# First two weights in quarters on the ScalarE queue, last output product on VectorE, two W_out pieces noted later

## The chip, the cores and the metric

One NeuronCore of a Trainium2 chip runs the whole program; the other cores are not used. The metric is the device time of one execution in microseconds (us). A profiled execution gives the trace that the tables below come from. TensorE is called PE here, its weight loads PEld, VectorE DVE, ScalarE ACT, GpSimd POOL and SyncE SP. A name with a q behind it (SPq, ACTq) is the queue side of that engine: instructions that issue a DMA. Line numbers L... are those of the kernel before.

## The reference, cut to what matters

Two transformer blocks run one after the other on x of 512 tokens by 1024 channels, fp32. Sizes of the gated feed-forward are 1024 to 2816 and back, those of the squared-ReLU one 1024 to 4096 and back.

```
def swiglu_ffn(x, w_gate, w_up, w_down):
    return (jax.nn.silu(x @ w_gate) * (x @ w_up)) @ w_down

def first_block(x, ...):
    x = x + 0.5 * swiglu_ffn(rmsnorm(x, ffn1_norm), ffn1_w_gate, ffn1_w_up, ffn1_w_down)
    x = x + hybrid_mixer(rmsnorm(x, mix_norm), ...)
    x = x + 0.5 * swiglu_ffn(rmsnorm(x, ffn2_norm), ...)
    return rmsnorm(x, final_norm)

def second_block(x, ...):
    h = rmsnorm_2(x, norm_mix_pre)
    ...
    mixed = jnp.concatenate([o_diff, o_mlstm], axis=-1) @ w_out
    x = x + rmsnorm_2(mixed, norm_mix_post)
    h = rmsnorm_2(x, norm_mlp_pre)
    u = jnp.square(jax.nn.relu(h @ w_up))
    return x + rmsnorm_2(u @ w_down, norm_mlp_post)
```

The change touches three places: the very first products (x @ ffn1_w_gate and x @ ffn1_w_up of the first block), the sum with w_out of the second block, and the last lines, rmsnorm_2(u @ w_down, norm_mlp_post) and the final sum.

## The kernel before

**Products.** Every fp32 product of two matrices is made of three products of the rounded type fp32r: high part by high part, low by high, high by low. So every operand is split in two. For a weight, ACT copies the raw tile `wraw` into `whi` and DVE subtracts to get `wlo` (`split`); for an activation ACT makes `xh` and DVE `xl`. One weight tile is 128 partitions by 1024 numbers (512 KB). There are 3 raw buffers (`R_BUFS`) and 4 split ones (`W_BUFS`); the list `L` (`plan`) holds all weight tiles in the order in which they are used, `w_load` issues their loads on SP's queue and `w_pump` (L448) notes the splits of tile i and the load of tile i + 3. The first two tiles, i = 0 (gate) and i = 1 (up), are split in two halves each (`step = m // 2 if i < 2`).

**Order of work.** The program is not issued as it is written. Every operation is noted (`Program.note`), and `issue` then plans: a list scheduler with estimated costs runs 60 sweeps forwards and backwards with some noise, keeps the best plan, and sends the operations to the engines sorted by planned start. Each engine then runs its own list strictly in order, and waits only where an operation's inputs are not ready or its buffer is still in use. A DMA is such an operation too, in the list of the engine on whose queue it is issued. All noted operations have the line of one helper, L232, in the profile, so they are told apart by their tiles here. DMA completions are counted in 8 semaphores (DMAHW0 to DMAHW7 below) that SP's and ACT's DMAs take by turns in issue order; a DMA that takes one again first waits until the former DMA of that semaphore has landed.

**The head** (L580 to 590 and `first_norm`). x comes in 8 pieces m of 128 channels (256 KB each, `XT<-x`); the gain of the first norm comes as `rows1` on ACT's queue. POOL builds the identity; PE makes 8 transposes of it and one of rows1. For every x piece, PE makes 4 transposes into a bank, ACT makes xh, DVE xl, and ACT or DVE copies the piece to X. The products of the first feed-forward need xh, xl of a piece and whi, wlo of the weight. The norm's scale is put in later, so the products need not wait for it.

```
for half in range(2):
    for m in range(4 * half, 4 * half + 4):
        load_x(m)
        if m == 4 * half:
            for i in range(2):
                k = slice(m, m + 4)
                self.sp.dma_start(self.w_view(self.raw[i], i)[:, k, :], self.L[i][1][:, k, :])
```

**The mLSTM heads** (L1231 to 1235). `scores(h)` and `value(h)` make head h; `o2a(j)` is the share of the diff-attention heads in the j-th pieces of the sum with w_out. These pieces are filler for PE between the heads.

**The tail** (`mlp_phase`, L1338 on). The last half of the output is made for one block of 128 tokens after the other, t = 0 to 3; the last block is cut into two pieces of 256 columns (p1, p2). `post` adds a piece to y (DVE), squares and sums it (ACT) and multiplies it by the gain (POOL). Then a short chain of 128x1 operations makes the norm's factor (cv on DVE, Ln and Exp on ACT, ct, ct, a2f on DVE), and DVE makes the last sum, `XT<-X,a2f,XT`, which SP stores.

Of the kernel before, what the change touches and what calls it, by code (L numbers as in the profile page):

```python
# [13 lines left out]
ALU = mybir.AluOpType  # L14
# [5 lines left out]
NT = 4  # L20
KD = 8
# [293 lines left out]
class Kern:  # L315
# [132 lines left out]
    def w_pump(self, upto):  # L448
        while self.w_split < min(upto + 1, len(self.L)):
            i = self.w_split  # L450
            self.w_load(i + R_BUFS)
            m = self.L[i][2] * self.L[i][3]
            step = m // 2 if i < 2 else m
            for c in range(0, m, step):
                c = slice(c, c + step)
                self.split(self.wh[i % W_BUFS][:, c], self.wl[i % W_BUFS][:, c], self.raw[i % R_BUFS][:, c])
            self.w_split += 1
            self.w_load(self.w_split + R_BUFS)
# [91 lines left out]
    def setup(self):  # L550
        tc, I, ctx = self.tc, self.I, self.ctx
        cp = ctx.enter_context(tc.tile_pool(name="cp", bufs=1))
        pp = ctx.enter_context(tc.tile_pool(name="pp", bufs=1, space=bass.MemoryType.PSUM))
        self.B = [pp.tile([P, 512], F32, name=f"bank{i}") for i in range(8)]
        self.mmb = Rot(self.B)
        dp = ctx.enter_context(tc.tile_pool(name="dp", bufs=1, space=bass.MemoryType.DRAM))
        self.tape = dp.tile([8, 16, 384], F32, name="tape")

        T = lambda name, shape, dt=F32: cp.tile(shape, dt, name=name)
        self.w_init(cp)  # L560
        self.X, self.XT = T("X", [P, KD, S]), T("XT", [P, NT, D])
        self.xh, self.xl = T("xh", [P, KD, S], F32R), T("xl", [P, KD, S], F32R)
        self.xs = [(self.xh[:, m, :], self.xl[:, m, :]) for m in range(KD)]
        self.ident, self.onesr = T("ident", [P, P]), T("onesr", [P, P], F32R)
        self.hm2 = T("hm2", [P, 2])
        self.rows1, self.rows, self.cols = T("rows1", [8, P]), T("rows", [NROW, P]), T("cols", [P, 8 + NROW])
        self.rcol = T("rcol", [P, NT])
        self.cv, self.ct, self.cr = (T(n, [P, 16]) for n in ("cv", "ct", "cr"))
        self.gfp = T("gfp", [P, KD])
        self.rsb, self.acc = T("rsb", [P, S]), T("acc", [P, S])  # L570
        self.sqh, self.sql = T("sqh", [P, S], F32R), T("sql", [P, S], F32R)
        self.sq = Rot([T(f"sq{i}", [P, S]) for i in range(2)])

        def load_x(m):
            self.sp.dma_start(self.XT[:, :, m * P:(m + 1) * P],
                              I["x"][0][:, m * P:(m + 1) * P].rearrange("(t p) c -> p t c", p=P))
        self.ac.dma_start(self.rows1, I["ffn1_norm"][0].rearrange("(r c) -> r c", c=P))
        self.po.memset(self.ident, 1.0)
        for s in (1, -1):
            self.po.affine_select(out=self.ident, in_=self.ident, pattern=[[s, P]], base=0, channel_multiplier=-s,  # L580
                                  compare_op=ALU.is_ge, fill=0.0)
        for half in range(2):
            for m in range(4 * half, 4 * half + 4):
                load_x(m)
                if m == 4 * half:
                    for i in range(2):
                        k = slice(m, m + 4)
                        self.sp.dma_start(self.w_view(self.raw[i], i)[:, k, :], self.L[i][1][:, k, :])
        self.w_dma = 2
        self.w_load(R_BUFS)  # L590
        self.prog.table(LN_EXP)
        self.act(self.onesr, self.ident, AF.Copy, scale=0.0, bias=1.0)
        self.ci = {"g1": 0}
        r = 0
        for name, src, n in [
            ("gm", I["mix_norm"][0], 8), ("g2", I["ffn2_norm"][0], 8),
            ("gf", I["final_norm"][0], 8), ("gp", I["norm_mix_pre_2"][0], 8), ("gu", I["norm_mlp_pre_2"][0], 8),
            ("psc", I["pool_scale"][0], 4), ("cb", I["conv_b_2"][0], 4), ("dn", I["diff_norm_2"][0], 1),
        ]:
            self.po.dma_start(self.rows[r:r + n, :], src.rearrange("(r c) -> r c", c=P))  # L600
            self.ci[name] = 8 + r
            r += n
        self.po.dma_start(self.rows[r:r + 16, :], I["conv_w_2"][0].rearrange("j (r c) -> (j r) c", c=P))
        self.ci["cw"] = 8 + r
        r += 16
        self.po.dma_start(self.rows[r:r + 4, :], I["mlstm_norm_2"][0])
        self.ci["ln"] = 8 + r
        r += 4
        for nm, key in (("qn", "q_norm"), ("kn", "k_norm")):
            for d in range(2):  # L610
                self.po.dma_start(self.rows[r:r + 1, d * 64:(d + 1) * 64], I[key])
            self.ci[nm] = 8 + r
            r += 1
        assert r == NROW
        self.po.dma_start(self.hm2, I["k_hm2"])
# [514 lines left out]
    def mlstm_phase(self):  # L1130
        I = self.I
        with self.mem.scope() as T:
# [22 lines left out]
            for t in range(NT):  # L1155
                b = self.bank()
# [15 lines left out]
            def o2a(i):  # L1172
                w = self.W(("o2A", i))
                for hf in range(2):
                    b = self.bank()
                    self.fgroup(b, w, o_x, hf * P)
                    self.act(y[:, 2 * i + hf, :], b, AF.Copy)
# [53 lines left out]
                self.split(*hls[i][1], self.mk[:, i, :])  # L1231
            scores(0), mo(0), mo(1), mo(2), mo(3), value(0)
            scores(1), o2a(0), o2a(1), value(1)
            scores(2), o2a(2), o2a(3), value(2)
            scores(3), value(3)
            self.y = y

    def mlp_phase(self):
        I = self.I
        X, y = self.X, self.y  # L1240
        with self.mem.scope() as T:
            uh, ul = T([P, 8, S], F32R), T([P, 8, S], F32R)
            rr = Rot([T([P, S]) for _ in range(2)])
            gp = T([P, D])
# [12 lines left out]
            b = self.bank()  # L1257
# [5 lines left out]
            for a in range(2):  # L1263
                cols = slice(a * H2, (a + 1) * H2)
                acc = self.acc[:, cols]
                for m in range(KD):
                    b = self.bank()
# [3 lines left out]
                b = self.bank()  # L1271
# [3 lines left out]
                for m in range(KD):  # L1275
                    t, xm = tmp.next(), X[:, m, cols]
# [21 lines left out]

            y = X[:].rearrange("p m s -> p (m s)").rearrange("p (t d) -> p t d", t=NT)

            def post(t, cs_, b, part):

                yt = y[:, t, cs_]
                self.tt(yt, b, yt, ALU.add)
                self.act(junk[:, cs_], yt, AF.Square, accum_out=ss[:, part, t:t + 1])
                self.tt(yt, yt, gp[:, cs_], ALU.mult, self.po)

            us = [(uh[:, m, :], ul[:, m, :]) for m in range(8)]
            for c in range(4):
# [9 lines left out]
                for m in range(lead, 8):  # L1319
                    b = self.bank()  # L1320
# [17 lines left out]
            for t in range(NT):  # L1338
                cuts = [(S, S)] if t < NT - 1 else [(S, H2), (S + H2, H2)]
                for i, (c0, n) in enumerate(cuts):  # L1340
                    b = self.bank()[:, :n]
                    self.tgroup(b, ww, us, t, slice(c0 - S, c0 - S + n))
                    post(t, slice(c0, c0 + n), b, 1 + i)
                    if len(cuts) > 1 and i == 0:
                        self.tt(s01[:, t:t + 1], ss[:, 0, t:t + 1], ss[:, 1, t:t + 1], ALU.add)
                cc = slice(t, t + 1)
                v, r, w = self.cv[:, cc], self.cr[:, cc], self.ct[:, cc]

                if len(cuts) > 1:
                    self.stt(v, ss[:, 2, cc], s01[:, cc], f5[:, cc], ALU.add, ALU.mult)  # L1350
                else:
                    self.stt(v, ss[:, 0, cc], ss[:, 1, cc], f5[:, cc], ALU.add, ALU.mult)
                self.act(tl[:, cc], v, AF.Ln, bias=eps)
                self.act(r, tl[:, cc], AF.Exp, scale=-0.5)
                self.act(yv[:, cc], r, AF.Copy, scale=v3[:, cc])
                self.stt(w, v, EPS, r, ALU.add, ALU.mult)
                self.stt(w, w, -0.5, r, ALU.mult, ALU.mult)
                self.stt(f4[:, cc], w, 1.5, yv[:, cc], ALU.add, ALU.mult)
                step = S if t < NT - 1 else H2
                for c0 in range(0, D, step):  # L1360
                    xt = self.XT[:, t, c0:c0 + step]
                    self.stt(xt, y[:, t, c0:c0 + step], f4[:, cc], xt, ALU.mult, ALU.add)
                    self.sp.dma_start(self.out[0][t * P:(t + 1) * P, c0:c0 + step], xt)
# [66 lines left out]
```

## Time and profile before

| | |
|---|---|
| median of 3 runs | 1520.19 us (1520.16 to 1520.71) |
| profiled execution, its own time | 1518.48 us |
| span of the profiled execution | 1516.8 us |
| PE busy | 1496.4 us, 99% of the span |
| DVE busy | 797.4 us, 53% |
| ACT busy | 629.5 us, 42% |
| POOL busy | 256.6 us, 17% |
| DMA | 156.10 MB, 103 GB/s on average |

The span goes from the first to the last instruction; the rest of the execution's time lies around it. Matmuls are pipelined: the duration of one record is longer than the distance to the next one, and a stretch of dense records counts as busy throughout. Idle time of an engine that nobody waits for costs nothing.

### The profile page before, as it was taken

To read this page: it belongs to the slowest core of one execution; us is meant where nothing else is said; L and a number is where in the kernel's file an instruction comes from. 1 tells how busy PE (TensorE), PEld (TensorE's weight loads), DVE (VectorE), ACT (ScalarE), POOL (GpSimd) and SP (SyncE) were. 2 spreads that over 40 slices of the span, in tenths; PEclk is the share of its full clock that TensorE was granted. 3 is DMA by queue.
4 is the path that set the end of the run, shared out by engine and by line. 5 is a ranking of instruction groups with operands and counts; after the bars stand their busy time and mean duration, and the time that the engine had idled before them with its cause. 6 is when DMAs were issued, how large, how long until landed. Compare 5 with 4: busy or idle time off the path is not lost. (4 is left out here: it accounts for less than half of the span.)

```text
span 1516.8 us, 18205 instructions
## 1 busy us (share of the span) xinstructions
PE 1496.4 (99%) x6931; PEld 1233.2 (81%) x6931; DVE 797.4 (53%) x1268; ACT 629.5 (42%) x1051; POOL 256.6 (17%) x234
## 2 busy tenths in 40 slices
PE   9999999999999999999999999999999999999997
PEld 7888888788878888888888888788898888888886
DVE  6442343346477884434443457888669424344335
ACT  6321332235348863312322355467555524132232
POOL 5120120113132121101300137110115000000002
PEclk9999999999999999999999999999999999999999
DMA  7333333433333433333433233645412233323321
GB/s 196 98 99 97 94 104 99 108 101 106 97 104 92 125 90 96 97 93 97 116 98 97 84 97 105 159 125 149 131 57 80 101 89 105 98 86 104 94 92 56
DMA packets 236327, 156.10 MB, mean 103 GB/s; under 512 B 7444, under 2 KB 214904, under 8 KB 236240
## 3 DMA queue, kind: packets, MB, share of 16 engines
q1 hardware_dynamic: 234368, 151.55, 35.1%
q0 software_dynamic: 1856, 3.40, 1.2%
q8 instruction: 54, 0.88, 0.3%
q14 instruction: 33, 0.27, 0.1%
q10 hardware_dynamic: 16, 0.00, 0.0%
HBM read 137.42 MB, written 2.29 MB: 92 GB/s over the span
## 5 line engine op out<-in xcount | busy, mean ns | idle before, releaser
L232 DVE TENSOR_TENSOR wlo<-wraw,whi 128x1024 fp32r<-128x1024 f32 (+2 forms) x258 | 321.6, 1247 | 427.2 <-ACT whi L232 332.5
L232 ACT ACTIVATE whi<-wraw 128x1024 fp32r<-128x1024 f32 (+2 forms) x258 | 267.8, 1040 | 512.2 <-PE bank L232 483.8
L232 PE MATMUL bank<-xl,whi 128*128 128x512 f32 (+1 forms) x1272 | 466.3, 384 | 1.0 <-DVE xl L232 0.8
L232 PE MATMUL bank<-xh,wlo 128*128 128x512 f32 (+1 forms) x1272 | 463.5, 384 | 0.6 <-DVE wlo L232 0.6
L232 PE MATMUL bank<-xh,whi 128*128 128x512 f32 (+1 forms) x1272 | 459.4, 383 | 1.0 <-ACT xh L232 0.6
L232 PEld LDWEIGHTS bank<-xl,whi 128*128 128x128 f32 x1272 | 238.8, 189 | 48.2 <-DVE xl L232 2.6
L232 PEld LDWEIGHTS bank<-xh,wlo 128*128 128x128 f32 x1272 | 239.4, 189 | 46.4 <-issue 1.0
L232 PEld LDWEIGHTS bank<-xh,whi 128*128 128x128 f32 x1272 | 238.6, 189 | 46.6 <-DVE a1r L232 0.8
L232 PE MATMUL bank<-whi,a2r 128*128 128x512 f32 (+1 forms) x528 | 155.7, 386 | 0.0
L232 PE MATMUL bank<-a1r,whi 128*128 128x512 f32 x480 | 151.1, 397 | 0.0
L232 PE MATMUL bank<-a2r,whi 128*128 128x512 f32 x416 | 130.5, 396 | 0.0
L232 PEld LDWEIGHTS bank<-whi,a2r 128*128 128x128 f32 x528 | 97.9, 188 | 20.4
L232 PEld LDWEIGHTS bank<-a1r,whi 128*128 128x128 f32 x480 | 89.3, 188 | 20.5 <-DVE X L232 0.2
L232 POOL TENSOR_TENSOR a1f<-a1f 128x512 f32<-128x512 f32 x40 | 60.2, 1505 | 263.7 <-DVE a1f L232 244.4
L232 POOL TENSOR_TENSOR a2f<-a2f 128x512 f32<-128x512 f32 x30 | 46.5, 1549 | 324.8 <-DVE a2f L232 254.6
L232 PE MATMUL bank<-wlo,a2r 128*128 128x512 f32 (+1 forms) x264 | 94.7, 385 | 0.0
L232 PEld LDWEIGHTS bank<-a2r,whi 128*128 128x128 f32 x416 | 77.6, 188 | 18.0
L232 PE MATMUL bank<-a1r,wlo 128*128 128x512 f32 x240 | 92.1, 398 | 0.0
L232 ACT ACTIVATE a2r<-a2f 128x512 fp32r<-128x512 f32 (+1 forms) x71 | 43.8, 620 | 104.2 <-POOL a2f L232 66.0
L232 PE MATMUL bank<-a2r,wlo 128*128 128x512 f32 x208 | 79.4, 396 | 0.0
L232 DVE TENSOR_TENSOR a2r<-a2f,a2r 128x512 fp32r<-128x512 f32 (+2 forms) x69 | 48.7, 708 | 51.7 <-ACT a2r L232 51.0
L232 POOL TENSOR_TENSOR acc<-acc,sq 128x512 f32<-128x512 f32 (+1 forms) x42 | 56.9, 1355 | 101.6 <-ACT sq L232 100.5
(243 smaller groups left out, 1476.7 us busy)
## 6 DMA issues: line engine op xcount, KB each, us to landing
wraw<-ffn_w_gate SPq DMA_DIRECT2D x43, 512.0 KB, 3.8
wraw<-ffn_w_up SPq DMA_DIRECT2D x43, 512.0 KB, 3.8
wraw<-w_in SPq DMA_DIRECT2D x40, 512.0 KB, 3.9
wraw<-ffn_w_down SPq DMA_DIRECT2D x32, 512.0 KB, 4.0
wraw<-w_up SPq DMA_DIRECT2D x32, 512.0 KB, 4.0
wraw<-w_down SPq DMA_DIRECT2D x32, 512.0 KB, 3.6
wraw<-w_out SPq DMA_DIRECT2D x16, 512.0 KB, 3.8
a2r<-a2r SPq DMA_DIRECT2D x60, 128.0 KB, 2.5
```

Of the source, the lines that this page charges most:

```text
L232: op.fn(*op.a, **op.k)
```

## The change

Three edits. The first two weight tiles are loaded in four quarters each (128x2x128, 128 KB) instead of two halves, and all eight quarters are issued on ACT's queue; the 8 pieces of x are alone on SP's queue until all are issued. The splits of these two tiles are made in quarters, too (128x256 instead of 128x512). In the last block of tokens the product with the gain is made by DVE instead of POOL. And `o2a(3)` is noted after head 3 instead of between `scores(2)` and `value(2)`.

```diff
@@ w_pump
             m = self.L[i][2] * self.L[i][3]
-            step = m // 2 if i < 2 else m
+            step = m // 4 if i < 2 else m
@@ the head
-        for half in range(2):
-            for m in range(4 * half, 4 * half + 4):
-                load_x(m)
-                if m == 4 * half:
-                    for i in range(2):
-                        k = slice(m, m + 4)
-                        self.sp.dma_start(self.w_view(self.raw[i], i)[:, k, :], self.L[i][1][:, k, :])
+        for m in range(KD):
+            load_x(m)
+            if m % 2 == 0:
+                for i in range(2):
+                    k = slice(m, m + 2)
+                    self.ac.dma_start(self.w_view(self.raw[i], i)[:, k, :], self.L[i][1][:, k, :])
@@ the mLSTM heads
-            scores(2), o2a(2), o2a(3), value(2)
-            scores(3), value(3)
+            scores(2), o2a(2), value(2)
+            scores(3), value(3), o2a(3)
@@ mlp_phase
-            def post(t, cs_, b, part):
+            def post(t, cs_, b, part, eng=None):
...
-                self.tt(yt, yt, gp[:, cs_], ALU.mult, self.po)
+                self.tt(yt, yt, gp[:, cs_], ALU.mult, eng or self.po)
...
-                    post(t, slice(c0, c0 + n), b, 1 + i)
+                    post(t, slice(c0, c0 + n), b, 1 + i, self.ve if t == NT - 1 else None)
```

Since the planner draws the whole program anew, the order of nearly every stretch moves a little. Two places matter here. The first is ACT's list at the start of the program. In the names, rows1 is the norm's gain, wraw0 and wraw1 the raw tiles of gate and up, whi0 and whi1 their high parts, onesr a tile of ones; in brackets stands what an instruction waits for (DMAHW counts landings, the others are engines). Before:

```order
L232 DMA rows1_90<-ffn1_norm 8x128
L232 ACT_TABLE_LOAD
L232 ACTIVATE onesr_88<-ident_87 128x128 [waits Pool_49]
L232 ACTIVATE xh_85<-bank5_66,cols_92 128x512 [waits DVE_49,PE_49]
L232 ACTIVATE xh_85<-bank6_67,cols_92 128x512 [waits PE_49]
L232 ACTIVATE whi0_75<-wraw0_72 128x512 [waits DMAHW4_49]
```

And now:

```order
L232 DMA rows1_90<-ffn1_norm 8x128
L232 DMA wraw0_72<-ffn1_w_gate 128x2x128
L232 DMA wraw1_73<-ffn1_w_up 128x2x128
L232 DMA wraw0_72<-ffn1_w_gate 128x2x128 [waits DMAHW1_49]
L232 DMA wraw0_72<-ffn1_w_gate 128x2x128 [waits DMAHW2_49]
L232 DMA wraw1_73<-ffn1_w_up 128x2x128 [waits DMAHW4_49]
L232 DMA wraw1_73<-ffn1_w_up 128x2x128 [waits DMAHW6_49]
L232 ACT_TABLE_LOAD
L232 ACTIVATE onesr_88<-ident_87 128x128 [waits Pool_49]
L232 ACTIVATE whi0_75<-wraw0_72 128x256
L232 ACTIVATE xh_85<-bank5_66,cols_92 128x512 [waits DVE_49,PE_49]
```

The first gate and up quarters stand there twice each (the second pair reads like the first). By the turns of the semaphores, DMAHW1 is the landing of x piece 0, DMAHW2 that of the first gate quarter, DMAHW4 that of the first up quarter and DMAHW6 that of x piece 2. All eight issues, the last four with a wait, now stand ahead of the table load and of everything that ACT computes.

The second is PE's list up to the first products, behind the transposes of the identity. Before, all of four x pieces stand ahead of the first product (bank5_66, bank6_67 and so on take the transposed pieces, bank0_61 and bank1_62 the sums of gate and up):

```order
L232 MATMUL bank_66<-ident,XT 128x128 x4
L232 MATMUL bank_67<-ident,XT 128x128 x4
L232 MATMUL bank_68<-ident,XT 128x128 x4
L232 MATMUL bank_65<-ident,XT 128x128 x4
L232 MATMUL bank_61<-xh,whi_75 128x512
```

Now:

```order
L232 MATMUL bank_66<-ident,XT 128x128 x4
L232 MATMUL bank_67<-ident,XT 128x128 x4
L232 MATMUL bank_61<-xh,whi_75 128x512
L232 MATMUL bank_62<-xh,whi_76 128x512
L232 MATMUL bank_68<-ident,XT 128x128 x4
L232 MATMUL bank_61<-xl,whi_75 128x512
```

Two pieces stand ahead of the first product and six behind it, where before it were four and four. On DVE at the end of the program, before:

```order
L232 TENSOR_TENSOR a2f_3584<-a2f_3584 128x1 [waits Activation_49]
L232 TENSOR_TENSOR X_83<-bank3_64,X_83 128x256 [waits PE_49]
L232 SCALAR_TENSOR_TENSOR cv_94<-a2f_3584 128x1 [waits Activation_49]
L232 SCALAR_TENSOR_TENSOR ct_95<-cv_94,cr_96 128x1 [waits DVE_49,Activation_49]
L232 SCALAR_TENSOR_TENSOR ct_95<-ct_95,cr_96 128x1 [waits DVE_49]
```

Now, with the two products with the gain among them:

```order
L232 TENSOR_TENSOR a2f_3596<-a2f_3596 128x1 [waits Activation_49]
L232 TENSOR_TENSOR X_83<-X_83,a2f_3596 128x256 [waits DMASW5_49,DVE_49]
L232 TENSOR_TENSOR X_83<-bank3_64,X_83 128x256 [waits PE_49]
L232 SCALAR_TENSOR_TENSOR cv_94<-a2f_3596 128x1 [waits Activation_49]
L232 TENSOR_TENSOR X_83<-X_83,a2f_3596 128x256 [waits DVE_49]
L232 SCALAR_TENSOR_TENSOR ct_95<-cv_94,cr_96 128x1 [waits DVE_49,Activation_49]
```

The product of p1 has come ahead of the sum of p2 (bank3_64), and the product of p2 between cv and ct.

## Rows read from the trace of the kernel before

**Rows 1.** Page: busy us of each engine, share of the span, instructions.

```profile
PE 1496.4 (99%) x6931; PEld 1233.2 (81%) x6931; DVE 797.4 (53%) x1268; ACT 629.5 (42%) x1051; POOL 256.6 (17%) x234
```

**Rows 2.** What PE waited for: engine, line, releaser, total us, times, longest.

```profile
PE bank L232 <- DMA a1r<-a1r: 2.8, 2, 2.0
...
PE bank L232 <- DMA XT<-x: 1.1, 1, 1.1
```

**Rows 3.** Timeline of PE in the head: start us, us, instruction, [idle before].

```profile
1.79 1.97 PE L232 MATMUL bank<-ident 128*128 128x128 f32 x8 [1.79 <-POOL ident L232]
...
3.89 3.09 PE L232 MATMUL bank<-ident,XT 128*128 128x128 f32 x12
8.09 0.63 PE L232 MATMUL bank<-ident,XT 128*128 128x128 f32 x4 [1.11 <-DMA XT<-x]
8.47 0.47 PE L232 MATMUL bank<-xh,whi 128*128 128x512 f32 x1
```

**Rows 4.** Timeline of ACT in the head.

```profile
0.80 0.62 ACTq L232 DMA_DIRECT2D rows<-ffn_norm  x1
1.46 1.28 ACT L232 ACT_TABLE_LOAD   x1 [1.46 <-PEq L1418]
2.75 0.31 ACT L232 ACTIVATE onesr<-ident 128x128 fp32r<-128x128 f32 x1
5.04 0.69 ACT L232 ACTIVATE xh<-bank,cols 128x512 fp32r<-128x512 f32 x1 [1.98 <-PE bank L232]
...
6.96 0.63 ACT L232 ACTIVATE whi<-wraw 128x512 fp32r<-128x512 f32 x1
```

**Rows 5.** Timeline of SP's queue in the head.

```profile
0.81 1.53 SPq L232 DMA_DIRECT2D XT<-x  x3
2.38 0.51 SPq L232 DMA_DIRECT2D wraw<-ffn_w_gate  x1
...
5.07 1.04 SPq L232 DMA_DIRECT2D wraw<-ffn_w_up  x1
```

**Rows 6.** The issue of x piece 2 alone (1.9 to 2.3 us): to landing.

```profile
L232 SPq DMA_DIRECT2D XT<-x x1: 507/507/507, 1.8 to 1.8; - x1
...
DMA to landing us min/median/max: 4.0/4.0/4.0
```

**Rows 7.** Stretches of the head: busy per engine, PE clock, DMA share, GB/s.

```profile
3.00:4.00 1.00, 1.00 (x6) 0.65 (x5) 0.00 (x1) 0.07 (x1) 1.00 (x3) 1.00 1.02 287
...
7.00:8.00 1.00, 0.00 (x0) 0.00 (x0) 1.00 (x3) 1.00 (x2) 0.30 (x1) 1.00 1.17 333
...
10.00:12.00 2.00, 2.00 (x12) 1.70 (x11) 1.00 (x3) 1.57 (x3) 0.00 (x0) 1.00 1.21 290
```

**Rows 8.** Stretches around a wait of PE in the first block, same columns.

```profile
439.00:440.00 1.00, 0.24 (x1) 0.24 (x2) 0.00 (x0) 0.00 (x0) 0.06 (x1) 1.00 0.51 153
440.00:441.00 1.00, 1.00 (x4) 0.57 (x3) 0.71 (x3) 0.00 (x0) 0.00 (x0) 0.72 1.06 320
441.00:442.00 1.00, 1.00 (x3) 0.56 (x2) 0.08 (x1) 0.97 (x3) 0.00 (x0) 0.50 0.26 78
442.00:443.00 1.00, 1.00 (x3) 0.75 (x3) 0.99 (x3) 0.81 (x2) 0.00 (x0) 0.50 0.00 0
443.00:444.00 1.00, 1.00 (x4) 0.77 (x3) 0.42 (x3) 0.32 (x2) 0.00 (x0) 0.57 0.00 0
```

**Rows 9.** Timelines of DVE and POOL in the tail.

```profile
1508.63 0.42 DVE L232 TENSOR_TENSOR X<-bank,X 128x256 f32<-128x256 f32 x1
1509.62 0.78 DVE L232 SCALAR_TENSOR_TENSOR cv<-a2f 128x1 f32<-128x1 f32 x1 [0.58 <-ACT a2f L232]
1511.00 0.16 DVE L232 SCALAR_TENSOR_TENSOR ct<-cv,cr 128x1 f32<-128x1 f32 x1 [0.60 <-ACT cr L232]
...
1509.66 0.72 POOL L232 TENSOR_TENSOR X<-X,a2f 128x256 f32<-128x256 f32 x1 [0.34 <-ACT a2f L232]
```

## The prediction

> **What bounds the kernel now.** The first view to read is the busy time of the engines: PE is busy for 1496.4 of 1516.8 us, every other engine for little over half of the span or less [rows 1]. So the time is PE's work plus some 20 us in which PE has nothing to do, and an edit that takes no product away can only win or lose in those holes. The second view says who ends PE's waits: the largest is an attention DMA (2.8 us), which this change does not touch; the one that it does touch is x at the start, 1.1 us [rows 2]. The third is the head, engine by engine. PE starts at 1.79 on the identity, turns three x pieces without a gap from 3.89 to 6.98, waits 1.11 us for the fourth, and makes its first product at 8.47 [rows 3]. ACT issues one small DMA, loads its table until 2.74, makes the ones, and has its first xh at 5.04 and the first whi at 6.96 [rows 4]. ACT is thus ready early and waits for data. The data come at 287 to 333 GB/s with the DMA share at 1.0 to 1.2 from 3 us on [rows 7]: the head is bound by the loads, 2 MB of x mixed with 1 MB of the two weights, and what matters is which piece comes first. The fourth is the tail, where PE has ended and DVE and ACT finish one chain [rows 9].
>
> A measurement of this kernel tells 0.2%, 3.0 us, from no change.
>
> **The loads move to ACT's queue.** The eight quarter loads now stand ahead of ACT's table load, and the last four wait for landings; the last one waits for x piece 2. ACT runs its list in order: in the profile its table load starts at 1.46, just when its only DMA issue (0.80, 0.62 us) is over [rows 4]. So the path to the first product is: x piece 2 lands; last issue, 0.51 us as on SP [rows 5]; table load 1.28; ones 0.31; first whi, now half as wide, 0.33 (half of 0.63 with a little that is fixed); xh 0.69 [rows 4]; with the handing over 3.2 us in all. DVE and PE have nothing else to wait for there: two pieces of x are turned by then.
>
> When does piece 2 land? Now it is issued at 1.83 and lands 4.0 us later, at 5.83 [rows 5, 6]. Lower bound: ACT's queue takes nothing from SP's, it lands at 5.83 again, and the first product is at 9.0. Upper bound: all seven quarters issued before the last one (0.92 MB) and the three pieces (0.79 MB) come ahead of it; 1.7 MB at 290 GB/s from about 2.1 us, plus some 0.9 from the last byte to the landing (0.79 MB at about 280 from 2.1 end at 4.9, and it landed at 5.83), is 8.8, and the first product is at 12.0. I take an even split between two queues that both have work: SP alone from 2.1 to some 2.75, the first quarter being issued at 1.42, 0.6 us behind the first x piece; then 0.6 MB at half of 290 GB/s, 4.1 us; with 0.9 to the landing 7.75. That lies between the ends, and nothing in the rows puts one queue ahead of the other. First product at 10.95, **2.5 us later** than 8.47 [rows 3].
>
> The Trainium skill, "DMA: Bandwidth & Descriptors", section "Queues, rings and completion order", says that each DMA engine goes round the queues that have work for it, packet by packet. By that rule the split is even and piece 2 lands near 7.75; no run here shows two such queues beside each other.
>
> **Work left behind the first product.** Before, 16 of the 32 transposes of x stood ahead of the first product, now 8. The other 8 come between the products, each at the 0.12 us by which the four at 8.09 followed each other (0.63 less one's own 0.27, by three) [rows 3]: **0.9 us**, since PE waits either way before the first product. The xh and wlo that follow come from ACT and DVE at 0.7 us apiece and each feeds several products; the quarters and x pieces 3 to 7 have mostly landed by 11. I put later waits at nothing new (0 to 0.5 us); their cover is that the loads were due at a rate that has not changed, while PE comes 2.5 us later.
>
> **PE's clock.** At 437 to 440 PE waits, and after it works on, the granted clock goes to 0.72, 0.50, 0.50 and 0.57 in four stretches of 1 us [rows 8], that is to 1.2 of 2.4 GHz: 0.28, 0.50, 0.50 and 0.43 us are lost, together 1.7. In the head the clock column says 1.00 throughout, but the transposes from 3.89 took 3.09 for 12, twice the pace of those at 8.09, and before the first product PE had worked nearly without a gap from 1.79 to 6.98 [rows 3]. Now PE turns two pieces, until about 7 if they land late, and idles until 11. I take the loss of the wait at 437, **1.7 us**; bounds 0 (the clock is full as at 8.09 now) and 2.6 (half the clock from 11 for 5.2 us, as long as PE worked from 1.79 to 6.98).
>
> **The tail.** The two products with the gain took POOL 0.72 each; cv took 0.78 beside one of them and other 128x1 operations take 0.16 [rows 9]. On DVE the second product falls under ACT's Ln and Exp, between cv and ct (0.60 us of waiting). The first comes ahead of the sum of p2, and that sum is on the path: +0.33, a 128x256 operation of 0.42 with its overlap [rows 9]. If cv then takes 0.16, it is -0.6 + 0.3 = **-0.3 us**; bounds -0.6 and +0.4 (cv as long as now).
>
> **The W_out pieces and the redraw.** In the engines' lists the o2a(3) products stand at nearly the same place of PE's list as before: the planner had put them there by itself. So this edit is worth nothing, and its cover is that head 3 has filler either way. The rest of the program is redrawn without any change in kind; waits and stretches at half clock like that at 440 [rows 8] may come out 2 us either way. I take -0.3, as the norm's sums behind the second block's w_out come a few products earlier.
>
> **The sum.** +2.5 + 0.9 + 1.7 - 0.3 - 0.3 = +4.5 us. The profiled execution took 1518.48 for a span of 1516.8, 1.7 around it, so by it the time would be 1523.0; the median of the runs lies 1.7 higher, at 1520.19. Against that: **1524.7 us**.
>
> **The rivals.**
> 1. *Piece 2 lands as before and the clock stays up.* For: it is issued at the same time, and 0.8 MB of x are ahead of most quarters in the order of issue. Against: the rate is already full [rows 7]. The sum is +0.5 + 0.9 + 0 - 0.6 = +0.8, 1521.0. If only one of the two holds, it is +2.5 (clock lost) or +2.8 (clock kept): 1522.7 to 1523.0, still within 0.2%.
> 2. *The quarters come first.* ACT's queue wins; piece 2 lands at 8.8. +3.5 + 0.9 + 2.2 - 0.6 = +6, 1526.2.
> 3. *The other side: ACT's compute is not held by its DMA issues.* If the waits of the issues stayed in a queue of their own, the table would be loaded by 2.8 as now, the first gate quarter (0.13 MB) would be there with x piece 0, and the first product would follow xh of piece 0, near 6.0 (5.04 + 0.69 and the whi of a quarter [rows 4]): -2.5 + 0.9 - 0.6 = -2.2, 1518.0. It decides for the change where the first product comes before some 8.2 us (8.47 + 0.6 - 0.9). For it: a quarter is less to wait for than a half. Against: the table load began when the issue ended [rows 4], and SP's issues show their waits as time of the issue (1.04 instead of 0.51) [rows 5].
> 4. *The redraw.* One half-clock stretch more or less is 1.7 us [rows 8], with the wait ahead of it up to 4; alone it gives 1516 to 1524.
> 5. *The change does not do what it says:* for o2a(3) I hold it likely, see above.
>
> The Trainium skill, "DMA: Bandwidth & Descriptors", section "Issuing engines are not separate DMA queues", says that DMAs of several engines run on the same 16 engines and interleave, and that issuing from several saves only the time of the issue. By that rule the move buys only SP's issue time of four loads; the share of 1.0 to 1.2 in the rows agrees that there is no idle bandwidth to win.
>
> **How the numbers follow.** My forecast's mechanism (ACT held, piece 2 late, clock lost) 0.50; one of the two conditions missing 0.18; rival 1 alone 0.09; rival 2 0.13; rival 3 0.05; a redraw that outweighs all of it 0.05. With 2 us either way from the redraw, the first is over +3.0 in 0.77 of its cases, the second in 0.35, rival 1 in 0.1, rival 2 in 0.95; rival 3 and the last come out under -3.0 in half of theirs, and a few of the others do. That makes slower 0.59, within 0.2% 0.34, faster 0.07. The range: from 1519.5 (rival 1 with a good redraw) to 1528.0 (rival 2 with a bad one).
>
> **What would show it.** In the profile of the changed kernel: ACT's table load at 8 us rather than 1.46, with ACT's queue issuing until then, the last issue ending just behind the landing of x piece 2; PE idle from about 7 to 11, with ACT's xh as the releaser; a clock of 0.5 behind it; cv at 0.16 in the tail. A table load before 4 us would refute the forecast, as would a first product before 8.5. If the first product is at 11 and the time is still under 1520, the redraw has given back what the head lost, and the stretch at 437 or another like it must show it.

## The result, and the profile after

The changed kernel takes 1529.43 us (1528.60 to 1530.91, 4 runs) against 1520.45 us (1520.16 to 1521.45, 4 runs): ratio 1.0064, interval 1.0052 to 1.0076, so 8 to 11.5 us more. The forecast was 1524.7 us, in a range of 1519.5 to 1528.0. The direction was right, the forecast size (+4.5) is half of the measured one (+9), and the time lies 1.4 us above the range. The profiled execution took 1528.60 us for a span of 1526.9, 10.1 us longer than before.

The busy times on the page of the changed kernel answer to [rows 1]:

```profile
PE 1498.8 (98%) x6931; PEld 1234.9 (81%) x6931; DVE 802.8 (53%) x1274; ACT 628.0 (41%) x1055; POOL 254.0 (17%) x232
```

PE has the same 6931 matmuls and is busy 2.4 us longer; the other 7.7 us of the span are holes. The head, where the prediction put its sum, first on ACT [rows 4]:

```profile
0.80 0.63 ACTq L232 DMA_DIRECT2D rows<-ffn_norm  x1
1.47 0.41 ACTq L232 DMA_DIRECT2D wraw<-ffn_w_gate  x1
...
3.88 1.80 ACTq L232 DMA_DIRECT2D wraw<-ffn_w_gate  x2
7.11 0.90 ACTq L232 DMA_DIRECT2D wraw<-ffn_w_up  x2
8.04 1.28 ACT L232 ACT_TABLE_LOAD   x1 [8.04 <-DMA wraw<-ffn_w_up]
9.34 0.31 ACT L232 ACTIVATE onesr<-ident 128x128 fp32r<-128x128 f32 x1
...
9.86 0.67 ACT L232 ACTIVATE xh<-bank,cols 128x512 fp32r<-128x512 f32 x1
```

The table load stands at 8.04 instead of 1.46, behind the eight issues, and the profile names the landing of an up quarter as what ended its wait. PE in the same stretch [rows 3]:

```profile
3.90 2.35 PE L232 MATMUL bank<-ident,XT 128*128 128x128 f32 x8
10.58 1.22 PE L232 MATMUL bank<-xh,whi 128*128 128x512 f32 x2 [4.33 <-ACT xh L232]
11.60 1.05 PE L232 MATMUL bank<-ident,XT 128*128 128x128 f32 x4
```

Two pieces are turned, then PE waits 4.33 us for xh, and the first product comes at 10.58 instead of 8.47. The stretches behind it (columns as in [rows 7]) show the clock:

```profile
10.00:12.00 2.00, 1.42 (x4) 1.20 (x5) 1.85 (x4) 1.71 (x4) 0.00 (x0) 0.50 1.21 302
12.00:14.00 2.00, 2.00 (x9) 1.60 (x8) 1.49 (x3) 1.17 (x2) 0.00 (x0) 0.50 1.19 290
14.00:16.00 2.00, 2.00 (x8) 1.60 (x7) 0.95 (x3) 1.17 (x3) 0.00 (x0) 0.50 0.42 105
16.00:18.00 2.00, 2.00 (x14) 1.76 (x13) 1.53 (x4) 1.36 (x5) 0.00 (x0) 0.91 0.00 0
```

PE works at 1.2 of 2.4 GHz from its first product to about 16 us. The tail on DVE [rows 9]:

```profile
1519.15 0.43 DVE L232 TENSOR_TENSOR X<-X,a2f 128x256 f32<-128x256 f32 x1
1519.49 0.42 DVE L232 TENSOR_TENSOR X<-bank,X 128x256 f32<-128x256 f32 x1
1520.49 0.22 DVE L232 SCALAR_TENSOR_TENSOR cv<-a2f 128x1 f32<-128x1 f32 x1 [0.58 <-ACT a2f L232]
1520.62 0.42 DVE L232 TENSOR_TENSOR X<-X,a2f 128x256 f32<-128x256 f32 x1
1521.31 0.16 DVE L232 SCALAR_TENSOR_TENSOR ct<-cv,cr 128x1 f32<-128x1 f32 x1 [0.26 <-ACT cr L232]
```

cv takes 0.22 instead of 0.78 without POOL beside it; from the sum of p2 to the first ct it is 1.82 us instead of 2.37, and the gain product ahead takes 0.34 of that back. Last, what PE waited for (form of [rows 2]):

```profile
PE bank L232 <- ACT xh L232: 4.3, 1, 4.3
PE bank L232 <- DVE xl L232: 3.0, 2, 2.2
PE bank L232 <- DMA a2r<-a2r: 2.5, 2, 2.3
PE bank L232 <- DMA a1r<-a1r: 2.3, 3, 1.0
PE bank L232 <- ACT a2f L232: 2.0, 1, 2.0
...
PE bank L232 <- DVE rsb L232: 0.9, 1, 0.9
```

Of these only the first line belongs to the head. The ones for xl (of the norm ahead of the last feed-forward), a2r and a2f (of the second block's attention) and rsb (of a norm) lie far behind it, at 943 to 1158 us, where no edit stands. The line of a1r, in the first block, was as long before (2.8). The same waits in the kernel before, where rsb has no line:

```profile
PE bank L232 <- ACT a2f L232: 1.3, 1, 1.3
...
PE bank L232 <- DVE xl L232: 0.8, 4, 0.3
PE bank L232 <- DMA a2r<-a2r: 0.8, 1, 0.8
```

To see where the time went I went through each trace's matmuls and summed, over neighbours, the distance of their starts less the median distance for the same shape in the kernel before. This is an excess that includes waits and half clock, in us; the places are given in the time of the kernel before, shifted by the lateness of each kernel's first product. "1st" and "2nd" say whose lists PE has in the two parts of the program (the planner is called twice; the second part starts behind the first block's mixer). The places left out, 540 to 930 and 1000 to 1125, differ from before by 0.4 at most.

```
kernel                  lists 1st/2nd   head 25-540 930-960 960-1000 1125-1180 1180-end  sum
before                  before/before    4.5  14.3    0.7     3.7      6.4       1.5   37.2
changed                 changed/changed  9.9  12.8    2.1     5.9      7.3       3.6   47.4
tail_only               before/before    5.9  12.4    0.7     3.9      6.4       1.5   36.8
loads_only              changed/before   9.2  12.5    0.7     6.6      6.5       1.5   43.5
loads_only_again        changed/before   9.5  12.7    0.7     6.1      6.6       1.5   43.4
wout_only               before/changed   7.4  12.5    2.0     6.8      7.3       3.6   45.6
new_plan_loads_on_sp    changed/changed  6.0  12.2    2.0     5.7      7.3       3.6   43.0
old_plan_loads_on_act   before/before    9.3  12.4    0.7     3.7      6.4       1.6   40.1
old_plan_four_on_act    before/before    7.2  12.5    0.7     3.8      6.4       1.5   38.0
quarters_on_sp          own/before       7.0  10.8    0.7     4.3      6.4       1.5   36.4
before_seed2            own/own          7.4  12.0    3.2     6.4      6.9       1.4   43.3
before_seed3            own/own          4.4  14.0    2.8     8.0      7.3       1.4   44.4
after_seed2             own/own         10.4  12.4    0.8     6.7      7.5       2.3   46.2
```

The sums differ by 10.3 between the kernel before and the changed one, the spans by 10.1. Of that 5.4 are the head, 6.6 the four places of the second part, and -1.5 the stretch from 25 to 540. Each row is one execution: rows with the same lists differ by up to 2.9 in the head and by as much at 960 to 1000.

### The profile page after: what moved, and what is told of

Read it like the earlier page. It is cut to its first block, busy times and chain, and to the rows that moved or that the text cites. A ratio compares the mean times of both kernels' runs of the same rounds, so it can differ in the third digit from the quotient of the medians.

```text
span 1526.9 us, 18211 instructions
## 1 busy us (share of the span) xinstructions
PE 1498.8 (98%) x6931; PEld 1234.9 (81%) x6931; DVE 802.8 (53%) x1274; ACT 628.0 (41%) x1055; POOL 254.0 (17%) x232
## 4 chain that ended last, share of the span: by engine, by line
PE 89%; DVE 5%; DMA 2%; ACT 1%; POOL 1%; issue 1%; SPq 1%; ACTq 0%; DVEq 0%; POOLq 0%
PE bank L232 89%; DVE XT L232 1%; DVE X L232 1%; DVE a2f L232 1%; DMA a1r<-a1r 1%; SPq L232 1%; POOL a2f L232 0%; DMA a2f<-a2f 0%; DVE xl L232 0%; ACT a2f L232 0%; DVE wlo L232 0%; DVE a1f L232 0%; DMA a2r<-a2r 0%; DMA wraw<-ffn_w_up 0%; POOL a1f L232 0%
## 5 line engine op out<-in xcount | busy, mean ns | idle before, releaser
L232 DVE TENSOR_TENSOR wlo<-wraw,whi 128x1024 fp32r<-128x1024 f32 (+2 forms) x262 | 325.1, 1243 | 410.0 <-ACT whi L232 328.4
```

The costliest lines, as they stand in the source:

```text
L232: op.fn(*op.a, **op.k)
```

## The experiments

Four kernels at first: each edit by itself, and the changed kernel with one thing undone. Theory 1 was that two causes add up, the head and the order that the planner drew anew; theory 2 that all comes from the head; theory 3 that all comes from the second part.

**Each edit alone.** `loads_only` has the first edit, `wout_only` the third, `tail_only` the second; their diffs are those of the change.

> The first edit alone: eight quarter loads on ACT's queue, the splits of the first two weights in quarters. The lists of PE are those of the changed kernel for the first block up to the second feed-forward and those of the kernel before from there on. Theory 1 (two causes that add up: the head, and the order that the planner drew anew): the first product comes at 10.6 us and the head costs 5.4 us, as in the changed kernel; the rest of the first part gives back 1.7 us (the waits after the head of the changed kernel's first part sum to 12.9 us against 14.5 before); the second part is that of before. So +3.7 us, ratio 1.0024. Theory 2 (all of the loss is made by the head, and what is late there goes on as late transfers in the second part): +9 us, 1.006. Theory 3 (all of the loss stands in the second part, what the head loses is given back): 0.

> The third edit alone: o2a(3) noted after head 3. The first part of the program is that of before to the last instruction; the second part's lists are those of the changed kernel without its tail. Theory 1: the products themselves stand where they stood, but the note makes the planner draw the whole second part anew, and the waits in it sum to 24.4 us in the changed kernel against 18.2 before: +6 us, ratio 1.004, with the waits at the same places as there (rsb, a2r, a2f). Theory 2 (head only): 0, within 0.1%. Theory 3: +9 us.

> The second edit alone: the gain of the last token block on DVE. All lists of PE are those of before. Theories 1 to 3 agree on the forecast's term: cv takes 0.16 us instead of 0.78, the sum of p2 comes 0.33 later, -0.3 us, which a measurement can't tell from 0; in the profile the time from PE's last product to the end falls from 9.7 us to about 9.4. If cv still takes 0.8, it is +0.3.

Measured against before: loads_only 1.0044 (1.0032 to 1.0057), wout_only 1.0046 (1.0034 to 1.0059), tail_only 1.0003 (0.9994 to 1.0012). Of a time of 1519 us these are +6.7, +7.0 and +0.5. So the edit that I had put at nothing costs as much as the one that carried the forecast. PE's lists say how: with the third edit alone, the first part is that of before to the last product, and 2312 of the products of the second part stand at another place. (Its head in the table, 7.4, is that of another execution of the same lists.) wout_only's waits show the changed kernel's places without its head:

```profile
PE bank L232 <- DVE xl L232: 3.0, 2, 2.2
PE bank L232 <- DMA a2r<-a2r: 2.6, 2, 2.3
...
PE bank L232 <- DVE rsb L232: 0.9, 1, 0.9
```

loads_only came out 3 us over its expectation, and the three losses sum to more than the changed kernel's; both are taken up below. In tail_only the time from PE's last product to the end is 9.4 us instead of 9.7, as expected. Theories 2 and 3 fall, since the first and the third edit each lose alone.

**The loads back on SP, all else as changed.** Lists of computing instructions word for word those of the changed kernel; only the queue of the eight quarter loads is another.

```diff
                     self.ac.dma_start(self.w_view(self.raw[i], i)[:, k, :], self.L[i][1][:, k, :])
+                    self.prog.ops[-1].fn = self.sp.queue.dma_start
```

(The diff is cut: further lines see to it that these loads and x are issued ahead of everything else, in the order of the code, a pair of quarters behind each even piece of x.)

> The changed kernel with all of its lists on PE, ACT's compute, DVE and POOL, only the eight quarter loads are back on SP's queue, each pair behind an even x piece. Theory 1: ACT loads its table at 1.5 us; x piece 1 lands behind 0.8 MB, at 5.8, the first product comes near 6.5, 4 us before that of the changed kernel; the queue then feeds PE at the rate of the loads, so the head ends 4 to 7 us earlier than in the changed kernel, and 0 to 2 earlier than before. With the redrawn rest (+4.5) the kernel is at +2.5 to +4.5 us, ratio 1.002 to 1.003. Theory 2 (all from the head): -1 to 0. A rival to the queue as the cause in the head (the quarters themselves, or PE's new order there): the first product stays at 10 us or later and the ratio at 1.006.

Measured: 1.0038 (1.0025 to 1.0050), +5.8 us. In the head PE waits for x piece 1 only, which 0.5 MB stand ahead of:

```profile
7.12 1.11 PE L232 MATMUL bank<-ident,XT 128*128 128x128 f32 x4 [2.12 <-DMA XT<-x]
7.89 1.20 PE L232 MATMUL bank<-xh,whi 128*128 128x512 f32 x2
```

The first product comes at 7.89 (expected 6.5). The head gives 3.9 us back in the table; by the ratios, 1.0064 less 1.0038, it is 4.0 us, 2.6 either way by the two intervals together. The second part's excess stays. So the queue costs about 4 us, and the rest of the loss is not in the loads.

**The loads on ACT, all lists as before.** The counterpart: the plan of the kernel before is kept to the last product, and only these loads are issued elsewhere, eight on ACT or, in a second kernel, the four whose issues wait for no landing on ACT and the other four on SP.

```diff
                         self.sp.dma_start(self.w_view(self.raw[i], i)[:, k, :], self.L[i][1][:, k, :])
+                        wd[half, i] = self.prog.ops[-1]
...
+            return sc.dma_start(self.w_view(self.raw[i], i)[:, k, :], self.L[i][1][:, k, :])
...
+            return self.sp.queue.dma_start(self.w_view(self.raw[i], i)[:, k, :], self.L[i][1][:, k, :])
```

(The diff is cut: the half loads are noted as before, and at issue each is replaced by its quarters; `sc` is ACT's queue. The last line is that of the second kernel, for the four on SP.)

> The kernel before with all its lists on PE, DVE, POOL and ACT's compute; only the first two weights are loaded in eight quarters on ACT's queue, in the change's order of issue, x alone on SP's. Theory 1 (head and redraw add up; the head's loss is ACT held by its issues): ACT's table load at 8 us, first product at about 12 (xh of piece 0 comes before whi in this order, and 16 transposes stand ahead), a stretch at half clock behind it, the rest as before: +3.5 to +5 us, ratio 1.0023 to 1.0033. Rival (the loss of the loads came from the planner's new order of the head, not from the queue): the head as before, within 1.001. Rival (what is late in the head goes on through the program): over +6, ratio over 1.004.

> As old_plan_loads_on_act, but only the four quarters whose issues wait for no landing stay on ACT's queue; the other four are on SP's queue, between the x pieces. All lists of computing instructions are those of before. Theory 1 (ACT is held by the issues that wait for landings): ACT's table load starts at 3.5 us instead of 7.5, the first xh is ready before 6.5, and the first product waits for x piece 3, which shares the queues with four quarters: 9 to 10 us; the head costs 0 to 1.5 us, ratio 1.000 to 1.001. Rival (two queues beside each other are the cost, not the waits): as old_plan_loads_on_act, 1.0018 or more, first product near 10.8.

Measured: 1.0018 (1.0009 to 1.0027) with eight, 1.0003 (0.9993 to 1.0012) with four. With eight the first product came at 10.82 (expected about 12). ACT with eight:

```profile
6.57 0.90 ACTq L597 DMA_DIRECT2D wraw<-ffn_w_up  x2
7.49 1.28 ACT L232 ACT_TABLE_LOAD   x1 [7.49 <-DMA XT<-x]
```

And with four:

```profile
2.98 0.52 ACTq L597 DMA_DIRECT2D wraw<-ffn_w_up  x1
3.54 1.28 ACT L232 ACT_TABLE_LOAD   x1 [3.54 <-issue]
```

Two queues beside each other cost nothing that can be measured. With the issues that wait it is 2.7 us (1.4 to 4.1), somewhat less than the 3.5 to 5 expected; the two intervals just overlap, and the second kernel also has another order on SP's queue, so the waits are the likely price here, not a proven one. With four, the first product still came at 10.60, as x piece 3 landed late, but all of PE's transposes ahead of it were done and the clock was up by 13 us. The time of the first product by itself is thus a poor measure of the head; what counts is how much work is left behind it, and at which clock it is done.

**A new draw with no edit.** Only the number that starts the planner's noise is changed.

```diff
-        rng = random.Random(1)
+        rng = random.Random(2)
```

> The kernel before with no edit but the number that starts the planner's noise (2 instead of 1): the same operations, both parts drawn anew. Theory 1 (a new draw alone moves the time by several us): it differs from before by more than 2 us either way, with the differences at the norms and the attention's DMA round trips, not in the products. Rival (draws are worth the same, and the note of o2a(3) costs 6 us by what it moves): within 0.1% of before.

> As before_seed2 with the number 3. Theory 1: again more than 2 us from before, and from before_seed2, either way. Rival: within 0.1%. If the spacing of the products of the last phase (229 ns before, 233 ns in the kernels with the new second part) is a matter of the draw, it is one or the other here, too.

> The changed kernel with the planner's noise started at 2: the same three edits, both parts drawn anew. Theory 1 (the draw makes most of the loss, and the draw of before is a good one): between 1.003 and 1.009 of before, with the first product near 10.5 us and the half clock behind it. Rival (the noted place of o2a(3) or the tail costs in itself, whatever the draw): it is at 1.006 again, and the same waits stand at rsb and a2r; below 1.002 neither holds, and the draw alone decides.

Measured: 1.0044 (1.0030 to 1.0058) and 1.0061 (1.0047 to 1.0075) for the kernel before with the numbers 2 and 3, 1.0043 (1.0029 to 1.0057) for the changed kernel with 2. A draw alone moves this kernel, by +7 and +9 us in the two tried, and not either way as expected. The changed kernel with 2 is no slower than the kernel before with 2 (1.0044). The second part of the program was drawn in four other ways here (once by the third edit), and all four are slower at 960 to 1000 us and at 1125 to 1180 us, three also at 930 to 960. (960 to 1000 alone proves little: loads_only has 6.1 to 6.6 there with the old order.) The waits of before_seed3 are the same kind as the changed kernel's:

```profile
PE bank L232 <- DVE xl L232: 2.9, 3, 2.6
...
PE bank L232 <- DVE rsb L232: 2.2, 1, 2.2
PE bank L232 <- ACT a2f L232: 2.1, 1, 2.1
PE bank L232 <- DVE sq L232: 2.1, 2, 1.2
```

The rival, that the noted place of o2a(3) costs in itself, is not needed: draws without it lose as much. It also can't make most of the loss: ACT copies the two sums of o2a(3) out at 1119.80 and 1122.63 us before and at 1125.17 and 1128.11 in wout_only, so at 930 to 1000 us, where wout_only has 4.4 of its excess, these products are still more than 100 us off and the note acts through the plan alone. For the 3 us from 1125 on the rival isn't excluded, since that edit was not tried in the old draw.

The planner doesn't see any of this. The estimate by which it keeps its best plan (`best` in `issue`, worked out from the kernels' sources without a run) is 895.6 to 895.8 us for the second part in all of these orders, and for the whole program 0.9 us less in the changed kernel than in the one before. Among orders that it holds equal, the kernel before has the best of the five that were run.

**Quarters without the queue.** The first edit with `self.sp` for `self.ac`, noted so that the planner knows it, and the second edit.

> The first two edits without the queue: quarters of the first two weights, noted on SP's queue in the same places of the code, the gain of the last block on DVE, o2a(3) where it was. The second part's lists are those of before, the first part is drawn anew with quarters on SP. Theory 1: ACT is free, the first product waits for x pieces 0 to 2 and one gate quarter (0.9 MB), near 7 to 8 us, one before that of before; -1 to +1 us, plus what the draw of the first part gives (2 us either way). Rival (smaller pieces cost in themselves, by eight more issues and landings): the first product at 9 or later and +3 us.

Measured: 1.0002 (0.9993 to 1.0011). The first product comes at 7.33, 1.1 us before that of the kernel before; half clock until about 11.5 takes that back. Quarters cost nothing, and win nothing. No kernel of this study beats the one before; this one, tail_only and old_plan_four_on_act equal it.

**loads_only again.**

> loads_only once more, for its profile. It took 6.7 us more than before where its head explains 3 to 4; in its profile the waits between 960 and 1000 us came to 6.6 us against 3.7 to 4.3 in the other kernels with the same lists there. If that is a matter of one execution, the profile now shows about 4 us there and the ratio falls towards 1.003; if the first part's new order brings it about, 6 to 7 us stand there again and the ratio is 1.004 again.

Measured: 1.0034 (1.0021 to 1.0048), both runs together about 1.0039, +5.9 us. Its second part has the lists of before, but both profiles show 6 to 7 us at 960 to 1000 instead of 3.7 to 4.3. PE waits there for ACT's a2f, once: 2.9 and 2.5 us of excess, against 1.5 in before, 1.8 in old_plan_loads_on_act and 2.2 in quarters_on_sp. Behind this wait the clock falls in both profiles of loads_only, in the first as follows (columns as in [rows 7]):

```profile
991.00:992.00 1.00, 1.00 (x5) 0.90 (x6) 0.62 (x2) 0.83 (x3) 0.00 (x0) 0.63 0.85 197
992.00:993.00 1.00, 1.00 (x6) 0.91 (x4) 0.67 (x5) 0.81 (x2) 0.00 (x0) 0.50 0.30 66
993.00:994.00 1.00, 1.00 (x6) 0.90 (x5) 0.29 (x2) 0.99 (x3) 0.00 (x0) 0.50 0.00 0
994.00:995.00 1.00, 1.00 (x8) 1.00 (x6) 0.00 (x0) 0.34 (x1) 0.00 (x0) 0.66 0.00 0
```

In old_plan_loads_on_act the same stretch stays at 1.00:

```profile
990.00:991.00 1.00, 1.00 (x8) 0.92 (x7) 0.90 (x3) 0.71 (x4) 0.00 (x0) 1.00 0.86 199
991.00:992.00 1.00, 1.00 (x9) 0.96 (x9) 0.56 (x4) 1.00 (x3) 0.00 (x0) 1.00 0.03 8
```

So half a us to one more of waiting is followed by 1.7 us lost to half clock (the shares missing from 1.00 in these four stretches). Why that wait is longer in both profiles of loads_only, whose instructions there are those of before, stays open. This place also accounts for most of why the edits do not add up: loads_only pays 2.6 us there, wout_only 3.1, and the changed kernel once 2.2, so 3.5 of the some 4 us that the single losses sum to above the changed kernel's.

## Why the prediction was half right

**ACT held by its issues: right.** It is shown twice, by old_plan_loads_on_act (in) and new_plan_loads_on_sp (out). The Trainium skill, "DMA: Bandwidth & Descriptors", section "Anatomy of one DMA — SWDGE (gpsimd) path", says of DMAs issued by GpSimd that "any semaphore wait happens on the issuing sequencer before dispatch"; the trace shows the same for ACT's issues, with the table load at 8.04. The planner, which put all eight ahead of the table load, knew little of this: in the kernel's source, `cost` counts a DMA's issue on ACT as 60 ns, where a quarter's took 370 to 530 ns here, and the plan has nothing of the landings that an issue waits for by the turns of the semaphores. The first product came at 10.58 where 10.95 was forecast, though not quite by the path named: x piece 2 landed at 6.85 (5.0 us behind its issue at 1.83), inside the bounds of 5.83 and 8.8 and before the 7.75 of an even split. What came last was the first up quarter, issued at 1.90 and landed 5.2 us later, at 7.1, which the seventh issue waited for; after it two issues of 0.45 instead of one of 0.51. One reading was wrong: rival 3 took SP's issue of 1.04 us as one that shows its wait. The two issues of x ahead of it, at 3.48 and 4.19 us, wait for no landing and took 0.67 and 0.83; and in the changed kernel the four issues on ACT that do wait took 0.37 to 0.49 each, with the wait as a gap ahead of them (5.68 to 7.11 ahead of the seventh).

**The clock: right mechanism, size beyond its bound.** Half clock from 10.58 to about 16 lost 0.7, 1.0, 1.0 and 0.2 in the four stretches, 2.9 us, not 1.7; the upper bound was 2.6. Against the one profile of before the head's sum still comes out: 2.1 us later, 0.9 of turned work moved behind, and 2.4 more of excess behind the first product (3.0 against 0.5) are the 5.4 of the table, where 5.1 were forecast. (The first transposes, "twice the pace" in the prediction, took twice the time.) What the forecast left out is that the kernel before pays some of this itself, and not the same in each execution: the same lists have a head of 4.5, 5.9 and 7.4 us in three profiles (before, tail_only, wout_only), with a first product at 8.5 to 9.2 and the clock up between 8 and 15 us. The profile that I worked from was the best of the three, which was luck. By the times of the runs the head costs 2.7 us (old_plan_loads_on_act) to 4.0 (new_plan_loads_on_sp), and not the 2.5 + 0.9 + 1.7 = 5.1 of the sum, which were taken from one execution.

**The tail: right, and too small to see.** -0.3 was forecast; 1.82 us instead of 2.37, less 0.34, is -0.2; the ratio can't tell it from 1.

**The redraw: wrong; this is the step that failed.** The prediction said of the third edit that "this edit is worth nothing" and of the redraw "I take -0.3", 2 us either way. The third edit alone measured +7.0 us (5.2 to 9.0). The 24 products of o2a(3) did stay where they were (2494 to 2539 in the planned list of the second part before, 2500 to 2540 now); that the rest of the program is redrawn was said, too. What failed is the price: I took the kernel's order as a middling one, which a new one may beat or not. The four other orders of the second part lose at the same few places, up to 2.5 us at 930 to 960, 2.0 to 4.3 at 960 to 1000 and 0.5 to 1.1 at 1125 to 1180. Those are where PE waits on a chain of other engines (rsb and the norm's xl on DVE, the attention's round trips a2r, a2f), and part of it is half clock behind a wait. That the new orders are slower there because they have these chains a few products later is my reading; no run moved one chain alone. 2.1 of the changed kernel's 6.6 us in the second part are no wait at all but a spacing whose cause is open (last section). Rival 4 had a mean of nothing and a chance of 0.05 to outweigh all; with the +5.1 that the table gives for the redraw (6.6 - 1.5) in place of -0.3 the sum would have been near 1530.

## What to carry to other kernels

Where a planner orders the program, an edit has two prices: what it does where it stands, and a new draw of everything that is planned with it. The second can be priced with no edit at all, by another start of the planner's noise; here that gave +7 and +9 us, as much as or more than any edit moved the time, and to judge an edit by itself its operations have to be moved inside the old plan. And a DMA on a computing engine's queue costs that engine its issue and every landing that the issue waits for: here four issues that wait for nothing ahead of ScalarE's first work cost nothing to measure, and eight of which the last four wait cost 2.7 to 4 us.

## What the runs showed beside that

The products of the last phase (u by w_down) are slower in every kernel with the changed second part. The records of them are longer. The page of wout_only has

```profile
L232 PE MATMUL bank<-whi,a2r 128*128 128x512 f32 (+1 forms) x528 | 156.3, 389 | 0.0
L232 PE MATMUL bank<-wlo,a2r 128*128 128x512 f32 (+1 forms) x264 | 94.4, 389 | 0.0
```

and that of tail_only

```profile
L232 PE MATMUL bank<-whi,a2r 128*128 128x512 f32 (+1 forms) x528 | 155.7, 386 | 0.0
L232 PE MATMUL bank<-wlo,a2r 128*128 128x512 f32 (+1 forms) x264 | 94.7, 385 | 0.0
```

Start to start it is 233 ns instead of 229, evenly over the last three quarters of the phase; on average over its some 735 products of 512 columns it is 232.7 instead of 229.3, 2.5 us, which is about the 2.1 by which the last column but one of the table differs. before_seed2 and before_seed3 have 229, and after_seed2 has 233 in the third quarter and 229 in the second and the fourth. The cause was not found.

And one long wait can cost more than itself: the clock falls after some waits and not after others of the same length. At the same product, ahead of a2r at 970 to 974 us, the changed kernel and wout_only both have 2.5 us of excess; behind it the granted clock stays at 1.00 in the changed kernel, and in wout_only it is at 0.50 for about 3 us. So the same list of products can differ there by some 1.6 us between two executions.
